# Subtracting a group mean, DMA-bound: adjacent groups loaded in 50688-byte pieces instead of one group at a time

## The chip, the cores and the metric

The kernel runs on one core of one Trainium2 chip. The metric is the device time of one execution in microseconds (us), as the median of several runs. Faster or slower needs 2%. The span of a profile is the profiled execution alone and lies 1.7 to 2.2 us under the device time of the same run in the cases quoted here.

## The reference

```python
x = randn(8, 4096, 2112)            # float32, 276.8 MB
x_r = x.reshape(8, 1024, 4, 2112)
pooled = x_r.mean(axis=2)           # mean of four adjacent rows
upsampled = repeat(pooled, 4, axis=1)
return x - upsampled
```

Every element is read once and written once, with about two additions an element in between.

## The kernel before

A group is four adjacent rows of 2112 floats, 33792 bytes. A tile holds one group in each of 128 partitions, 4.325 MB, and there are 64 tiles ("groups" from here on). Six slots of that size form a ring. SyncE issues the loads, ScalarE's queue issues the stores, VectorE computes. No tensor is multiplied.

```python
def reduce_tile(b, landed):
    rows = slots[b].rearrange("p (f d) -> p f d", f=STRIDE)
    s = s_ps if b % 2 else s_sb
    for f in range(1, STRIDE):                       # three additions, 128x2112
        first = rows[:, 0, :] if f == 1 else s[:]
        add = nc.vector.tensor_add(out=s[:], in0=first, in1=rows[:, f, :])
        # ... waits: the load for f == 1, the step before it otherwise
    sub = nc.vector.scalar_tensor_tensor(            # rows = rows - s / 4, 128x8448, in place
        out=rows, in0=s[:, None, :].to_broadcast([P, STRIDE, D]),
        scalar=-1.0 / STRIDE, in1=rows, op0=mult, op1=add)
    # ...

for k in range(n):                                   # n = 64
    b, lap = k % SLOTS, k // SLOTS                   # SLOTS = 6
    load = nc.sync.dma_start(out=slots[b][:], in_=xg[k * P:(k + 1) * P])
    if lap:
        load._wait_ge(store_sems[b], 16 * lap)       # the slot's last store has landed
    load.then_inc(load_sems[b], 16)
# ... VectorE: a loop over the slots ...
for k in range(n):
    b = k % SLOTS
    store = nc.scalar.dma_start(out=og[k * P:(k + 1) * P], in_=slots[b][:])
    store._wait_ge(done_sem, k + 1)
    store.then_inc(store_sems[b], 16)
```

Of the kernel before, what the change touches and what calls it, by code (L numbers as in the profile page):

```python
# [1 line left out]

# [4 lines left out]

STRIDE = 4
SLOTS = 6  # L10
PAD = 224


@with_exitstack
def kernel(
    ctx: ExitStack,
    tc: tile.TileContext,
    x: bass.AP,
    out: bass.AP,
):  # L20






    nc = tc.nc
    B, S, D = x.shape
    P = nc.NUM_PARTITIONS
    W = STRIDE * D  # L30
    G = (B * S) // STRIDE
    assert S % STRIDE == 0 and G % P == 0
    n = G // P

    xg = x.rearrange("b (g f) d -> (b g) (f d)", f=STRIDE)
    og = out.rearrange("b (g f) d -> (b g) (f d)", f=STRIDE)
    f32 = mybir.dt.float32

    pad_pool = ctx.enter_context(tc.tile_pool(name="pad", bufs=1))
    io_pool = ctx.enter_context(tc.tile_pool(name="io", bufs=1))  # L40
    sum_pool = ctx.enter_context(tc.tile_pool(name="sum", bufs=1))
    psum_pool = ctx.enter_context(
        tc.tile_pool(name="psum", bufs=1, space=bass.MemoryType.PSUM)
    )
    pad_pool.tile([P, PAD], f32, name="pad")
    slots = [io_pool.tile([P, W], f32, name=f"slot{b}") for b in range(SLOTS)]
    s_sb = sum_pool.tile([P, D], f32, name="s_sb")
    s_ps = psum_pool.tile([P, D], f32, name="s_ps")

    load_sems = [tc.alloc_semaphore(f"load{b}") for b in range(SLOTS)]  # L50
    store_sems = [tc.alloc_semaphore(f"store{b}") for b in range(SLOTS)]
    step_sem = tc.alloc_semaphore("step")
    done_sem = tc.alloc_semaphore("done")

    adds = STRIDE - 1

    def reduce_tile(b, landed):
        rows = slots[b].rearrange("p (f d) -> p f d", f=STRIDE)
        s = s_ps if b % 2 else s_sb
        done = b * adds  # L60
        for f in range(1, STRIDE):
            first = rows[:, 0, :] if f == 1 else s[:]
            add = nc.vector.tensor_add(out=s[:], in0=first, in1=rows[:, f, :])  # L63
            if f == 1:
                add._wait_ge(load_sems[b], landed)
            else:
                add._wait_ge(step_sem, done + f - 1)
            add.then_inc(step_sem)
        sub = nc.vector.scalar_tensor_tensor(  # L69
            out=rows,  # L70
            in0=s[:, None, :].to_broadcast([P, STRIDE, D]),
            scalar=-1.0 / STRIDE,
            in1=rows,
            op0=mybir.AluOpType.mult,
            op1=mybir.AluOpType.add,
        )
        sub._wait_ge(step_sem, done + adds)
        sub.then_inc(done_sem)

    assert SLOTS % 2 == 0  # L80
    laps, rest = divmod(n, SLOTS)
    with tc.tile_critical():  # L82
        for k in range(n):
            b, lap = k % SLOTS, k // SLOTS
            load = nc.sync.dma_start(out=slots[b][:], in_=xg[k * P:(k + 1) * P])
            if lap:
                load._wait_ge(store_sems[b], 16 * lap)
            load.then_inc(load_sems[b], 16)

        with nc.vector.Fori(0, laps) as lap:  # L90
            landed = nc.vector.to_reg(16 * lap + 16)
            for b in range(SLOTS):
                reduce_tile(b, landed)
            nc.vector.wait_ge(step_sem, SLOTS * adds).then_inc(step_sem, -SLOTS * adds)
        for b in range(rest):
            reduce_tile(b, 16 * (laps + 1))

        for k in range(n):
            b = k % SLOTS
            store = nc.scalar.dma_start(out=og[k * P:(k + 1) * P], in_=slots[b][:])  # L100
            store._wait_ge(done_sem, k + 1)
            store.then_inc(store_sems[b], 16)


    for k in range(n - SLOTS, n):
        total = nc.gpsimd.to_reg(16 * (k // SLOTS + 1))
        tc.keep_in_program_order(nc.gpsimd.wait_ge(store_sems[k % SLOTS], total))


# [1 line left out]
_INS = ['x']  # L111
_OUTS = [((8, 4096, 2112), 'float32')]


# [23 lines left out]
```

## Time and profile before

| | before |
|---|---|
| median time | 1284.73 us (5 runs, 1284.56 to 1285.19) |
| span of the profile | 1283.3 us |
| VectorE busy | 1026.5 us, 80% |
| bytes moved | 553.66 MB, mean 431 GB/s |
| a load lands after / a store lands after | 60.1 us / 43.5 us |

The page's groups of VectorE give the cost of its work (columns: line, engine, operation, operands, shapes, count, then total us, mean ns of one, and the idle time ahead of them with what ended it):

```profile
L69 DVE SCALAR_TENSOR_TENSOR slot<-s_sb,slot 128x8448 f32<-128x8448 f32 x32 | 286.7, 8958 | 1.1
...
L63 DVE TENSOR_TENSOR s_sb<-slot 128x2112 f32<-128x2112 f32 x32 | 75.5, 2358 | 123.7 <-DMA slot<-in_x_dram 123.7
```

One subtraction takes 8.96 us and one addition 2.36 us. Nearly all of VectorE's idle time stands ahead of the first addition of a group and is ended by a load. That is what a kernel looks like whose DMA sets the pace.

### The profile page before, as it was taken

Reading aid. Unit: us, or ns where it says so; the run is one execution under the profiler, and the core shown is the slowest. Engines: PE = TensorE matmul, PEld = TensorE weight load, DVE = VectorE, ACT = ScalarE, POOL = GpSimd, SP = SyncE. Lnnn points to the kernel's source line nnn. Section 1 sums busy time; section 2 is a strip of 40 time slices with the busy share of each in tenths; the row PEclk is TensorE's granted clock in tenths of the full one; section 3 lists DMA queues with packets and bytes.
Section 4 is the critical chain, followed back from the end, with each engine's and each line's share of the span. In section 5 each row is a group of like instructions: output and inputs, shape, how many; then the busy total and the mean of one; then the engine's idle time right before and its main releaser. Section 6 shows DMA issues by size and latency. Waiting matters only on the chain.

```text
span 1283.3 us, 483 instructions
## 1 busy us (share of the span) xinstructions
DVE 1026.5 (80%) x256; POOL 0.2 (0%) x4
## 2 busy tenths in 40 slices
DVE  5998788787887877878778787787877878878785
POOL 0000000000000000000000000000000000000000
DMA  9999999999999999999999999999999999999999
GB/s 404 420 436 429 434 437 434 427 437 436 427 436 437 434 427 437 436 427 436 437 433 428 437 436 426 437 437 433 428 437 434 428 437 437 432 429 437 434 427 404
DMA packets 18432, 553.66 MB, mean 431 GB/s; under 512 B 2048, under 2 KB 2048, under 8 KB 2048
## 3 DMA queue, kind: packets, MB, share of 16 engines
q1 hardware_dynamic: 9216, 276.83, 50.1%
q10 hardware_dynamic: 9216, 276.83, 50.0%
HBM read 276.82 MB, written 276.82 MB: 431 GB/s over the span
## 4 chain that ended last, share of the span: by engine, by line
DVE 73%; another core or an unknown queue 24%; DMA 1%; issue 1%; DVEq 0%; SPq 0%
DVE slot L69 38%; DVE s_ps L63 18%; DVE s_sb L63 18%; DMA slot<-in_x_dram 1%; DVEq L90 0%; SPq L133 0%; SPq L82 0%
## 5 line engine op out<-in xcount | busy, mean ns | idle before, releaser
L69 DVE SCALAR_TENSOR_TENSOR slot<-s_sb,slot 128x8448 f32<-128x8448 f32 x32 | 286.7, 8958 | 1.1
L69 DVE SCALAR_TENSOR_TENSOR slot<-s_ps,slot 128x8448 f32<-128x8448 f32 x32 | 286.6, 8957 | 1.1
L63 DVE TENSOR_TENSOR s_sb<-slot 128x2112 f32<-128x2112 f32 x32 | 75.5, 2358 | 123.7 <-DMA slot<-in_x_dram 123.7
L63 DVE TENSOR_TENSOR s_ps<-slot 128x2112 f32<-128x2112 f32 x32 | 75.7, 2367 | 112.1 <-DMA slot<-in_x_dram 112.1
L63 DVE TENSOR_TENSOR s_ps<-s_ps,slot 128x2112 f32<-128x2112 f32 x64 | 151.4, 2366 | 2.2
L63 DVE TENSOR_TENSOR s_sb<-s_sb,slot 128x2112 f32<-128x2112 f32 x64 | 150.9, 2358 | 2.2
L122 POOL MEMSET const-bfloat16-1.0<- 128x1 bf16 x1 | 0.1, 102 | 0.0
L122 POOL MEMSET const-uint8-127<- 128x1 uint8 x1 | 0.1, 102 | 0.0
L122 POOL MEMSET const-float32-0.0<- 128x1 f32 x1 | 0.1, 99 | 0.2 <-issue 0.2
L122 POOL MEMSET const-float32-1.0<- 128x1 f32 x1 | 0.1, 99 | 0.0
## 6 DMA issues: line engine op xcount, KB each, us to landing
slot<-in_x_dram SPq DMA_DIRECT2D x64, 4224.0 KB, 60.1
out_dram<-slot ACTq DMA_DIRECT2D x64, 4224.0 KB, 43.5
```

The lines of the kernel that those rows point to most:

```text
L63: add = nc.vector.tensor_add(out=s[:], in0=first, in1=rows[:, f, :])
L69: sub = nc.vector.scalar_tensor_tensor(out=rows, in0=s[:, None, :].to_broadcast([P, STRIDE, D]), scalar=-1.0 / STRIDE, in1=rows, op0=mybir ...
L122: nc = _bacc.Bacc("TRN2", target_bir_lowering=False, num_devices=1)
```

## The change

Intent: fewer and larger load transfers. The first 54 groups are taken as 18 blocks of three adjacent groups, so that a partition's data of a block is 12 contiguous rows, 101376 bytes. A block is loaded as two pieces of six rows (50688 bytes a partition), but stored a group at a time. A piece ends in the middle of the second group, so a load must wait for two groups' stores. The last ten groups go one at a time as before. The diff, cut to its core:

```diff
+BLOCK = 3
+BLOCKS = 18
-    slots = [io_pool.tile([P, W], f32, name=f"slot{b}") for b in range(SLOTS)]
+    ring = io_pool.tile([P, SLOTS * W], f32, name="ring")
 # ... the access patterns of a block: 12 rows a partition ...
+    def block(h, landed):
+        base = h * rows_all
+        s0, s1 = sums[h], sums[1 - h]
+        group(s0, base, (load_sems[h][0], landed)).then_inc(done_sem)
+        add(s1, ring_rows(base + 4, 1), ring_rows(base + 5, 1))
+        nc.vector.wait_ge(step_sem, steps.count)
+        add(s1, s1[:], ring_rows(base + 6, 1), (load_sems[h][1], landed))
+        add(s1, s1[:], ring_rows(base + 7, 1))
+        subtract(s1, base + 4, STRIDE).then_inc(done_sem)
+        group(s0, base + 8).then_inc(done_sem)
-        for k in range(n):
-            b, lap = k % SLOTS, k // SLOTS
-            load = nc.sync.dma_start(out=slots[b][:], in_=xg[k * P:(k + 1) * P])
-            if lap:
-                load._wait_ge(store_sems[b], 16 * lap)
-            load.then_inc(load_sems[b], 16)
+        for b in range(BLOCKS):
+            h, lap = b % 2, b // 2
+            for e in range(2):
+                q = h * BLOCK + 2 * e
+                if lap and e == 0:
+                    nc.sync.wait_ge(store_sems[q], 16 * lap)
+                load = nc.sync.dma_start(
+                    out=ring_rows(h * rows_all + e * piece, piece),
+                    in_=xb[b][:, e * piece * D:(e + 1) * piece * D],
+                )
+                if lap:
+                    load._wait_ge(store_sems[h * BLOCK + 1 + e], 16 * lap)
+                load.then_inc(load_sems[h][e], 16)
+        for k in range(singles):
+            # ... ten single groups, loaded as before ...
 # ... the stores: one a group, in both parts ...
```

More of the change, by code (lines that the diff above doesn't have):

```diff
@@ L32 @@
     assert S % STRIDE == 0 and G % P == 0
-    n = G // P
-    xg = x.rearrange("b (g f) d -> (b g) (f d)", f=STRIDE)
-    og = out.rearrange("b (g f) d -> (b g) (f d)", f=STRIDE)
     f32 = mybir.dt.float32
+    singles = G // P - BLOCK * BLOCKS
+    laps = BLOCKS // 2
+    assert BLOCKS % 2 == 0 and SLOTS == 2 * BLOCK and singles >= SLOTS
+    rows_all = BLOCK * STRIDE
+    piece = rows_all // 2
+    xr = x.rearrange("b s d -> (b s) d")
+    orow = out.rearrange("b s d -> (b s) d")
+    cut = BLOCKS * P * rows_all
+    xb = xr[0:cut].rearrange("(n p r) d -> n p (r d)", p=P, r=rows_all)
+    ob = orow[0:cut].rearrange("(n p r) d -> n p (r d)", p=P, r=rows_all)
+    xs = xr[cut:B * S].rearrange("(n p f) d -> n p (f d)", p=P, f=STRIDE)
+    os_ = orow[cut:B * S].rearrange("(n p f) d -> n p (f d)", p=P, f=STRIDE)
     pad_pool = ctx.enter_context(tc.tile_pool(name="pad", bufs=1))
@@ L45, with ring_rows, add, subtract @@
     pad_pool.tile([P, PAD], f32, name="pad")
-    slots = [io_pool.tile([P, W], f32, name=f"slot{b}") for b in range(SLOTS)]
+    ring = io_pool.tile([P, SLOTS * W], f32, name="ring")
     s_sb = sum_pool.tile([P, D], f32, name="s_sb")
     s_ps = psum_pool.tile([P, D], f32, name="s_ps")
-    load_sems = [tc.alloc_semaphore(f"load{b}") for b in range(SLOTS)]
-    store_sems = [tc.alloc_semaphore(f"store{b}") for b in range(SLOTS)]
+    sums = [s_sb, s_ps]
+    load_sems = [[tc.alloc_semaphore(f"load{h}{e}") for e in "eo"] for h in range(2)]
+    sload = [tc.alloc_semaphore(f"sload{q}") for q in range(SLOTS)]
+    store_sems = [tc.alloc_semaphore(f"store{q}") for q in range(SLOTS)]
     step_sem = tc.alloc_semaphore("step")
     done_sem = tc.alloc_semaphore("done")
-    adds = STRIDE - 1
-    def reduce_tile(b, landed):
-        rows = slots[b].rearrange("p (f d) -> p f d", f=STRIDE)
-        s = s_ps if b % 2 else s_sb
-        done = b * adds
-        for f in range(1, STRIDE):
-            first = rows[:, 0, :] if f == 1 else s[:]
-            add = nc.vector.tensor_add(out=s[:], in0=first, in1=rows[:, f, :])
-            if f == 1:
-                add._wait_ge(load_sems[b], landed)
-            else:
-                add._wait_ge(step_sem, done + f - 1)
-            add.then_inc(step_sem)
+    def ring_rows(first, count):
+        return ring[:, first * D:(first + count) * D]
+    class Steps:
+        count = 0
+    steps = Steps()
+    def add(s, a, b, wait=None):
+        ins = nc.vector.tensor_add(out=s[:], in0=a, in1=b)
+        if wait is not None:
+            ins._wait_ge(*wait)
+        else:
+            ins._wait_ge(step_sem, steps.count)
+        ins.then_inc(step_sem)
+        steps.count += 1
+    def subtract(s, first, count):
+        rows = ring_rows(first, count).rearrange("p (f d) -> p f d", f=count)
         sub = nc.vector.scalar_tensor_tensor(
             out=rows,
-            in0=s[:, None, :].to_broadcast([P, STRIDE, D]),
+            in0=s[:, None, :].to_broadcast([P, count, D]),
             scalar=-1.0 / STRIDE,
@@ L76, in reduce_tile @@
         )
-        sub._wait_ge(step_sem, done + adds)
-        sub.then_inc(done_sem)
-    assert SLOTS % 2 == 0
-    laps, rest = divmod(n, SLOTS)
-    with tc.tile_critical():
-        for k in range(n):
-            b, lap = k % SLOTS, k // SLOTS
-            load = nc.sync.dma_start(out=slots[b][:], in_=xg[k * P:(k + 1) * P])
-            if lap:
-                load._wait_ge(store_sems[b], 16 * lap)
-            load.then_inc(load_sems[b], 16)
+        sub._wait_ge(step_sem, steps.count)
@@ new lines, in subtract, with group @@
+        return sub
+    def group(s, first, wait=None):
+        add(s, ring_rows(first, 1), ring_rows(first + 1, 1), wait)
+        for f in range(2, STRIDE):
+            add(s, s[:], ring_rows(first + f, 1))
+        return subtract(s, first, STRIDE)
+    def block(h, landed):
[8 more added lines that the diff above has]
+        group(s0, base + 8).then_inc(done_sem)
@@ new lines @@
+    with tc.tile_critical():
+        for b in range(BLOCKS):
[12 more added lines that the diff above has]
+        for k in range(singles):
+            q, lap = k % SLOTS, k // SLOTS
+            load = nc.sync.dma_start(out=ring_rows(q * STRIDE, STRIDE), in_=xs[k])
+            load._wait_ge(store_sems[q], 16 * (laps + lap))
+            load.then_inc(sload[q], 16)
@@ L90 @@
         with nc.vector.Fori(0, laps) as lap:
             landed = nc.vector.to_reg(16 * lap + 16)
-            for b in range(SLOTS):
-                reduce_tile(b, landed)
-            nc.vector.wait_ge(step_sem, SLOTS * adds).then_inc(step_sem, -SLOTS * adds)
-        for b in range(rest):
-            reduce_tile(b, 16 * (laps + 1))
-        for k in range(n):
-            b = k % SLOTS
-            store = nc.scalar.dma_start(out=og[k * P:(k + 1) * P], in_=slots[b][:])
+            steps.count = 0
@@ new lines @@
+            for h in range(2):
+                block(h, landed)
+            nc.vector.wait_ge(step_sem, steps.count).then_inc(step_sem, -steps.count)
+        steps.count = 0
+        for k in range(singles):
+            q, lap = k % SLOTS, k // SLOTS
+            group(sums[k % 2], q * STRIDE, (sload[q], 16 * (lap + 1))).then_inc(done_sem)
+        for k in range(BLOCK * BLOCKS + singles):
+            q = k % SLOTS
+            b, g = divmod(k, BLOCK)
+            if b < BLOCKS:
+                rows = ob[b][:, g * W:(g + 1) * W]
+            else:
+                rows = os_[k - BLOCK * BLOCKS]
+            store = nc.scalar.dma_start(out=rows, in_=ring_rows(q * STRIDE, STRIDE))
@@ L101 @@
             store._wait_ge(done_sem, k + 1)
-            store.then_inc(store_sems[b], 16)
-    for k in range(n - SLOTS, n):
-        total = nc.gpsimd.to_reg(16 * (k // SLOTS + 1))
+            store.then_inc(store_sems[q], 16)
+    for k in range(singles - SLOTS, singles):
+        total = nc.gpsimd.to_reg(16 * (laps + k // SLOTS + 1))
         tc.keep_in_program_order(nc.gpsimd.wait_ge(store_sems[k % SLOTS], total))
```

## The prediction

> **What bounds the kernel now.** I read the page first: the busy share of each engine, then the DMA row of the 40 slices, then the queues.
>
> ```profile
> DVE 1026.5 (80%) x256; POOL 0.2 (0%) x4
> DMA  9999999999999999999999999999999999999999
> DMA packets 18432, 553.66 MB, mean 431 GB/s; under 512 B 2048, under 2 KB 2048, under 8 KB 2048
> q1 hardware_dynamic: 9216, 276.83, 50.1%
> q10 hardware_dynamic: 9216, 276.83, 50.0%
> ```
>
> VectorE, the only computing engine, has a fifth of the span free. The 16 DMA engines have nothing free: the load queue (q1) and the store queue (q10) hold 50.1% and 50.0% of their time. 276.83 MB must come in and 276.83 MB go out, whatever the order. So the first question is whether the DMA engines ever run below their rate. I asked for the busy time and GB/s of five stretches of the span (columns: stretch, its us, DVE busy, POOL busy, clock, DMA share, GB/s):
>
> ```profile
> 3.00:28.00 25.00, 14.57 (x4) 0.00 (x0) 1.00 1.00 433
> 28.00:36.00 8.00, 7.93 (x4) 0.00 (x0) 1.00 0.95 355
> 36.00:136.00 100.00, 90.77 (x23) 0.00 (x0) 1.00 1.01 435
> 136.00:1236.00 1100.00, 884.35 (x222) 0.00 (x0) 1.00 1.00 433
> 1236.00:1276.00 40.00, 28.84 (x7) 0.00 (x0) 1.00 1.00 433
> ```
>
> Loads alone (3 to 28 us) run at 433 GB/s, loads with stores (136 to 1236) at 433, and the last stretch, nearly all stores, at 433. The rate doesn't depend on which queue has work, only on some queue having it. The one weak stretch is 28 to 36 us, when the first store starts: 8 x (433-355)/433 = 1.4 us by this coarse count (a packet falls into one stretch or the next), about 1.0 us by the packet records. All bytes at 433 GB/s take 553.66/0.433 = 1279 us (1277 if the unrounded rate is 433.5). The span is 1283.3. So everything that is not bytes at full rate is worth 4 to 6 us, under 0.5%.
>
> The packet records show how two queues share an engine. In the steady part a packet is one partition's row of 33792 bytes and takes 1.251 us, with loads alone or mixed; each engine moves one at a time and strictly alternates load, store, load, store. So the share is per packet, not per byte.
>
> Last, the DMA issues and the waits of VectorE:
>
> ```profile
> slot<-in_x_dram SPq DMA_DIRECT2D x64, 4224.0 KB, 60.1
> out_dram<-slot ACTq DMA_DIRECT2D x64, 4224.0 KB, 43.5
> DVE s_sb L63 <- DMA slot<-in_x_dram: 123.7, 30, 13.3
> DVE s_ps L63 <- DMA slot<-in_x_dram: 112.1, 30, 3.8
> ```
>
> A load lands 60.1 us after issue and a store 43.5 us, while one group moves in and out in 2 x 4.325 MB / 0.433 = 20.0 us: three loads and two stores are always queued. VectorE takes 3 x 2.36 + 8.96 = 16.05 us a group, then waits 3.8 us for a load. 60.1 + 16.05 + 43.5 = 119.7 us is six periods of 20 us: all six slots are in use, and the DMA sets the period. The chain of waits (73% VectorE) misleads here: VectorE lies on it because each store follows a subtraction, but it has 3.8 us of slack a group.
>
> **What the Trainium skill says.** "DMA: Bandwidth & Descriptors", section "Bandwidth", gives a ceiling of 435.2 GB/s for the 16 engines; the trace sits at 433, 0.5% under it. Section "Queues, rings and completion order" of the same page says each engine takes turns between the queues that have work, at packet granularity; the trace agrees, 1.251 us turns of one row each. Section "Rules for kernel authors" asks for 128 partitions and at least 1 MiB a DMA; before already moves 4.3 MB, so there is little left to gain from size. Section "Latency and other measured facts" warns of HBM rows at large power-of-two pitches. The new pitch is 3 x 33792 = 101376 bytes, no power of two; no run yet shows whether it matters.
>
> **The change part by part.**
> 1. Instructions. VectorE keeps 192 additions and 64 subtractions of the same shapes, 64 x 16.05 = 1027 us, and the stores stay 64 of 33792 bytes a partition. Loads go from 64 to 36 + 10. The program order shows no other work.
> 2. Load packets. 18 blocks x 128 x 2 = 4608 rows of 50688 bytes replace 6912 of 33792: 2304 fewer, 144 an engine. The worth of one: a row repeats every 33792 x 16 / 433.5 GB/s = 1.247 us; at the skill's 435.2 it would be 1.242. So at most 0.005 us a row (an estimate from that ceiling), 144 x 0.005 = 0.7 us saved.
> 3. Start. The first load is 1.5 groups, so VectorE starts at about 18 us instead of 13.3 and the first store at 34 instead of 29.5. Four pieces (60 us of loading) are queued from the start, so the DMA stays busy: cost 0.
> 4. Steady part, worked by hand with 10 us for a group and 15 us for a piece alone. While both queues have work a load turn is 1.87 us and a store turn 1.25 us: the loads get 60%, a piece takes 25 us, and in those 25 us one group is stored. A piece needs two groups' stores done before it is issued (pieces share the middle group). From about 82 us a block goes: first piece beside one store, 25 us; second piece beside the next store, 25 us; then no slot is free and the third store runs alone, 10 us; then the next first piece. 25 + 25 + 10 = 60 us for three groups, exactly 3 x 20. VectorE needs 48.2 of these 60. In the hand schedule a block's stores are ready 16, 39 and 55 us after its first piece has landed, but their turns on the queue come 60 us or later after it, so the store queue never runs dry. The load queue does, once a block for some 10 us, and the stores fill it at 433 GB/s. Cost in bytes: 0.
> 5. End. Ten single groups run as before, at 50:50. More stores are queued behind the loads here (about five against three), so the last subtraction is hidden; before also has no hole there (433 GB/s to 1276 us). Gain: 0.
> 6. Restarts of the load queue. This is the only new thing. Before never lets a queue run empty, and the single time that a queue starts beside a busy one, at 28 to 36 us, each engine shows two load packets stretched from 1.25 to about 1.4 to 2.2 us, together about 1.0 us. After restarts the load queue once in each of 16 blocks. If every restart costs that, 16 x 1.0 = 16 us, fully on the path because the DMA is the bound. If that microsecond belongs to the very first store only, it is 0.
>
> Sum: 1284.7 - 0.7 + 0 = 1284 without a restart cost, 1284.7 - 0.7 + 16 = 1300 with it in full.
>
> **The rivals.** (a) Pure conservation of bytes: nothing moves, 1284 us. For it: the rate is 433 in every mix. (b) Restart cost: 1292 to 1300; if the second piece also comes too late and the queue empties twice a block, 16 + 16 = 32 us, 1316. The store beside a piece starts about 2 us before it (issue to first byte is 1.4 us in the trace), and so finishes before it and frees the next piece just in time; I hold twice a block unlikely. (c) Larger pieces starve VectorE, and VectorE then starves the stores: against it, 48.2 of 60 us busy, and a backlog of stores; each store is ready some 40 us before its turn, so VectorE would have to be that late. (d) Larger packets are faster than 0.005 us a row: the ceiling allows at most 0.5%, 1278 us. (e) The 101376-byte pitch slows HBM: the trace has nothing of it; I give it a few per cent.
>
> **Range and chances.** I give (a) a little more than half and (b) most of the rest, perhaps with a partial cost; between 1284 and 1300 I put 1288, with 1281.5 to 1303 for 8 in 10. Faster by 2% (under 1259 us) would need more than the ceiling: 0.5%. Slower by 2% (over 1310.4) needs the double restart or a pitch effect: 5.5%. Within 2%: 94%.
>
> **What would show it.** Right: VectorE still 1026 us busy; load rows of 50688 bytes at about 1.87 us; GB/s of 433 in nearly every slice, and over a block of 60 us; waits of VectorE on loads in two sizes a block, some 5 and 7 us by hand; the load queue empty once a block. Restart cost: short dips of GB/s every 60 us, with load rows above 1.9 us right after each gap. Wrong: DMA share below 9 in the steady part (a hole), a block period well over 61 us, or a store row longer than 1.25 us in the mix (the pitch).

## The result, and the profile after

| | before | after |
|---|---|---|
| median time | 1284.73 us | 1285.80 us (5 runs, 1285.16 to 1285.90) |
| span of the profile | 1283.3 us | 1283.6 us |
| VectorE busy | 1026.5 us | 1023.1 us |
| a store lands after | 43.5 us | 55.5 us |
| first data packet to last, packet records | 1280.1 us | 1280.2 us |

The ratio of after to before is 1.0006, 95% interval 0.9994 to 1.0018. A ratio here is the mean time of one kernel's fast runs over that of the other's fast runs of the same rounds, so it is not quite the ratio of the medians. One core can't show the difference between two dies, so a run counts as slow only if it is over 1.5% above the fastest of its kernel; nothing in the comparison of the two kernels rests on such runs.

The page of the changed kernel, its VectorE row, its GB/s in 40 slices, its packets and its two data queues:

```profile
DVE 1023.1 (80%) x256; POOL 0.2 (0%) x4
GB/s 404 413 441 435 426 433 438 430 442 428 440 424 444 434 423 434 440 429 431 437 432 443 421 435 437 431 432 436 433 440 430 440 428 428 434 436 434 430 434 394
DMA packets 15841, 553.66 MB, mean 431 GB/s; under 512 B 1760, under 2 KB 1760, under 8 KB 1760
q1 hardware_dynamic: 6624, 276.83, 50.0%
q10 hardware_dynamic: 9216, 276.83, 49.9%
```

The load queue q1 has 6624 packets in place of 9216 for the same megabytes, and yet the mean rate is again 431 GB/s. The two lowest slices, 404 and 394, are the first and the last: the transfers begin in the one and run out in the other, before and after alike. The stretches of the span, cut as for before (the start comes later, since the first piece is larger):

```profile
34.00:42.00 8.00, 7.86 (x4) 0.00 (x0) 1.00 0.99 372
136.00:1036.00 900.00, 719.26 (x180) 0.00 (x0) 1.00 1.00 433
1036.00:1236.00 200.00, 173.75 (x43) 0.00 (x0) 1.00 1.01 434
1236.00:1276.00 40.00, 16.05 (x4) 0.00 (x0) 1.00 1.00 433
```

The blocks (136 to 1036 us), the single groups and the end all run at 433 to 434 GB/s. The weak stretch at the first store is still there. One block in mid run, cut at its own phases by hand:

```profile
496.00:506.00 10.00, 7.56 (x3) 0.00 (x0) 1.00 1.00 433
506.00:531.00 25.00, 22.07 (x5) 0.00 (x0) 1.00 1.00 433
531.00:556.00 25.00, 18.32 (x5) 0.00 (x0) 1.00 1.00 433
556.00:566.00 10.00, 8.11 (x3) 0.00 (x0) 1.00 1.00 433
```

In the two 10 us stretches the packet records hold almost no load packet: the load queue is dry and stores move alone. In the two 25 us stretches loads and stores are mixed. The rate is 433 GB/s in all four. VectorE's timeline of the next block, only the rows at which it waits (start, us, engine, line, operation, and in brackets the idle time with what ended it):

```profile
532.98 2.37 DVE L74 TENSOR_TENSOR s_ps<-ring 128x2112 f32<-128x2112 f32 x1 [4.81 <-DMA ring<-in_x_dram]
...
557.83 4.75 DVE L74 TENSOR_TENSOR s_sb<-s_sb,ring 128x2112 f32<-128x2112 f32 x2 [6.42 <-DMA ring<-in_x_dram]
...
593.15 2.36 DVE L74 TENSOR_TENSOR s_sb<-ring 128x2112 f32<-128x2112 f32 x1 [5.51 <-DMA ring<-in_x_dram]
```

A block waits twice, 4.8 us for its first piece and 6.4 us for its second, and the next block begins 593.15 - 532.98 = 60.2 us later. The issues of the DMA with their median time to landing:

```profile
out_dram<-ring ACTq DMA_DIRECT2D x64, 4224.0 KB, 55.5
ring<-in_x_dram SPq DMA_DIRECT2D x36, 6336.0 KB, 33.3
```

Before, three loads and two stores were queued. After, little more than one load is queued (33.3 us from issue to landing, of which a piece's own moving takes 25), and the waiting has shifted to the store queue, 55.5 us. The data wait in the ring in either case; only the place has changed.

### The profile page after: what moved, and what is told of

Its sections match the earlier page's. It is cut to its first block, busy times and chain, and to the rows that moved or that the text cites. A ratio compares the mean times of both kernels' runs of the same rounds, so it can differ in the third digit from the quotient of the medians.

```text
span 1283.6 us, 495 instructions
## 1 busy us (share of the span) xinstructions
DVE 1023.1 (80%) x256; POOL 0.2 (0%) x4
## 3 DMA queue, kind: packets, MB, share of 16 engines
q1 hardware_dynamic: 6624, 276.83, 50.0%
q10 hardware_dynamic: 9216, 276.83, 49.9%
## 4 chain that ended last, share of the span: by engine, by line
another core or an unknown queue 80%; DVE 9%; DMA 7%; SPq 1%; issue 0%; DVEq 0%
DVE ring L84 5%; DMA out_dram<-ring 4%; DMA ring<-in_x_dram 4%; DVE s_ps L74 2%; DVE s_sb L74 2%; SPq L119 1%; SPq L128 0%; SPq L118 0%; DVEq L106 0%; SPq L182 0%; SPq L112 0%
## 5 line engine op out<-in xcount | busy, mean ns | idle before, releaser
L84 DVE SCALAR_TENSOR_TENSOR ring<-s_sb,ring 128x8448 f32<-128x8448 f32 x32 | 286.7, 8958 | 1.1
L84 DVE SCALAR_TENSOR_TENSOR ring<-s_ps,ring 128x8448 f32<-128x8448 f32 x32 | 286.6, 8957 | 1.1
L74 DVE TENSOR_TENSOR s_sb<-s_sb,ring 128x2112 f32<-128x2112 f32 x64 | 150.9, 2358 | 53.8 <-DMA ring<-in_x_dram 51.8
L74 DVE TENSOR_TENSOR s_ps<-s_ps,ring 128x2112 f32<-128x2112 f32 x64 | 151.4, 2366 | 52.8 <-DMA ring<-in_x_dram 50.8
L74 DVE TENSOR_TENSOR s_sb<-ring 128x2112 f32<-128x2112 f32 x32 | 75.3, 2352 | 69.9 <-DMA ring<-in_x_dram 69.9
L74 DVE TENSOR_TENSOR s_ps<-ring 128x2112 f32<-128x2112 f32 x32 | 75.6, 2362 | 51.5 <-DMA ring<-in_x_dram 51.5
## 6 DMA issues: line engine op xcount, KB each, us to landing
out_dram<-ring ACTq DMA_DIRECT2D x64, 4224.0 KB, 55.5
ring<-in_x_dram SPq DMA_DIRECT2D x36, 6336.0 KB, 33.3
```

Of the source, the lines that this page charges most:

```text
L74: ins = nc.vector.tensor_add(out=s[:], in0=a, in1=b)
L84: sub = nc.vector.scalar_tensor_tensor(out=rows, in0=s[:, None, :].to_broadcast([P, count, D]), scalar=-1.0 / STRIDE, in1=rows, op0=mybir. ...
```

## The experiments

All kernels below start from one of the two kernels with a single edit more that is common to all: the last wait of GpSimd is written on constants. Packet figures are from the packet records of the profiled run. "Stretched" is the time by which packets exceeded the normal duration of their size, summed and divided by 16 engines; "idle" is the time with fewer than 16 packets in flight, counted for each missing packet and also divided by 16. A gap of a queue is counted from the start of its last packet to the start of the next, so that one packet's own 1.25 or 1.87 us is in it. Both kernels have little of either in the whole run: before 1.6 us stretched and 1.2 us idle, after 1.9 and 1.5.

### The changed kernel again

```diff
-        total = nc.gpsimd.to_reg(16 * (laps + k // SLOTS + 1))
-        tc.keep_in_program_order(nc.gpsimd.wait_ge(store_sems[k % SLOTS], total))
+            nc.gpsimd.wait_ge(store_sems[k % SLOTS], 16 * (laps + k // SLOTS + 1))
```

> The changed kernel again; only the last wait of GpSimd is written on constants (the register form is not accepted by the safety check). Theory A (the time is the bytes at the rate of the DMA engines plus a fixed head and tail): 1284 to 1286.5 us, ratio to before 1.000 to 1.001. Rival B (the half microsecond to one microsecond by which the changed kernel was slower is real and steady): ratio 1.0005 to 1.0010 again, with a start and a tail that each lose 0.2 to 0.4 us more in the packet records. Load packets of 50688 bytes at 1.872 us, none stretched at the 31 restarts of the load queue.

Measured: 1285.43 us against 1284.81, ratio 1.0004 (0.9991 to 1.0017). The start lost 0.25 us idle and 0.76 us stretched, the end 0.60 us idle; before has 0.13, 0.60 and 0.57. The median is again above before, here by 0.6 us, but the interval holds 1. In all four comparisons of this schedule (the first, this one, and below 20 blocks and one more addition) it is 0.6 to 1.1 us above, and every interval holds 1: the sign is a hint and not a finding. The larger end (0.94 us idle in the first profile) did not come again. The restarts of the load queue again have no stretched packets to speak of. The control agrees with theory A, and leaves B open: the time is the bytes, and a difference of half a microsecond can't be told from none.

### Every row its own transfer

```diff
-            load = nc.sync.dma_start(out=slots[b][:], in_=xg[k * P:(k + 1) * P])
+            for f in range(STRIDE):
+                c = slice(f * D, (f + 1) * D)
+                load = nc.sync.dma_start(out=slots[b][:, c], in_=xg[k * P:(k + 1) * P, c])
 # ... the same for the stores; counts of 16 become 64
```

> Before, with every load and store cut in four transfers of one 8448-byte row a partition: 65536 packets in place of 16384, 3072 more an engine, the same bytes. Theory A with a fixed cost a packet: from the two sizes measured (1.251 us for 33792 bytes, 1.872 us for 50688) the fixed part is 3 x 1.251 - 2 x 1.872 = 0.009 us, so 3072 x 0.009 = 28 us more, 1312 us; with 0.005 us as predicted, 15 us more, 1300 us. Rival: no fixed cost a packet, 1285 us.

Measured: 1304.39 us, ratio 1.0151 (1.0136 to 1.0166). The page's packets and the mid run of this kernel:

```profile
DMA packets 73732, 553.71 MB, mean 425 GB/s; under 512 B 8192, under 2 KB 8192, under 8 KB 8192
...
136.00:1236.00 1100.00, 871.27 (x219) 0.00 (x0) 1.00 1.01 428
```

The loss is spread over the whole run (428 in place of 433 GB/s), with no hole. 1304.39 - 1284.81 = 19.6 us over 3072 more packets an engine is 0.0064 us a packet, between the two figures expected. It includes four times as many semaphore packets. It also includes about 3 us that lie at the start and the end: in the steady part alone (100 to 1230 us, 427.6 against 433.1 GB/s by the packet records) the loss comes to 16.4 us for all bytes, 0.0054 us a packet. So the prediction's saving of 144 packets an engine is worth 0.8 to 0.9 us.

### Stores as pieces too

```diff
+        for b in range(BLOCKS):
+            for e in range(2):
+                store = nc.scalar.dma_start(out=ob[b][:, e * piece * D:(e + 1) * piece * D],
+                                            in_=ring_rows(h * rows_all + e * piece, piece))
+                store._wait_ge(done_sem, b * BLOCK + 2 + e)
 # ... and a load waits for the one store of its piece
```

> The changed kernel with its 18 blocks also stored as two 50688-byte pieces, so each load waits for one store. Theory A: 2304 fewer store packets, 144 an engine, at 0.005 to 0.009 us: 0.7 to 1.3 us less than the changed kernel, 1284 to 1285 us, no hole in the DMA row. Rival C (a store of a piece must wait for two groups, and the coarser stores starve the DMA): GB/s below 425 in slices of the steady part, 1300 us or more.

Measured: 1290.89 us median of six runs, but they are 1286.40, 1286.57, 1287.68, 1294.10, 1300.20 and 1302.35; ratio 1.0072 (1.0035 to 1.0109). The profiled run is one of the quick ones, 1286.57 us: 434 GB/s from 136 to 1036 us, no hole there, and 2.3 us idle at 1270 to 1273 us, where the last store waits for the last subtraction, which ends at 1272.1 us. Neither expectation came out. The saving did not show, and the profile can't say what the runs near 1300 us did. That stays open. It also shows that one program can vary by over 1% from run to run, which bears on the single runs below.

### One load at a time

```diff
+            if k:
+                nc.sync.wait_ge(load_sems[(k - 1) % SLOTS], 16 * ((k - 1) // SLOTS + 1))
             load = nc.sync.dma_start(out=slots[b][:], in_=xg[k * P:(k + 1) * P])
```

> Before, with each load issued only when the load ahead of it has landed, so the load queue runs empty 63 times while stores go on. Theory A (a queue may run empty as long as the other has work): 1285 to 1295 us, the upper end if both queues are sometimes empty at once. Rival D (each restart of a queue costs the engines about 1 us, as at the first store): 63 us more, about 1348 us, with stretched load packets after each gap.

Measured: 1354.55 us (1349.15 to 1362.98), ratio 1.0528 (1.0502 to 1.0554); the profile is of the slowest of the four runs, 1362.98. My theory missed, and the number is the rival's. The issues in the page show what I had overlooked:

```profile
slot<-in_x_dram SPq DMA_DIRECT2D x64, 4224.0 KB, 20.3
out_dram<-slot ACTq DMA_DIRECT2D x64, 4224.0 KB, 19.4
```

Not only the load queue but the store queue too is down to one transfer (19.4 us to landing against 43.5), so that both run dry again and again. The profiled run's 77.6 us between first and last packet beyond before split into 49.7 us stretched (51.3 - 1.6) and 27.6 us idle (28.8 - 1.2, of which 10.9 lie at the end, where nothing hides the last subtraction and store). The largest clusters of stretched packets, 1.2 to 1.35 us an engine each, lie some 4 us after a store has started, where the next load joins it; others are smaller; in the changed kernel 16 long restarts have next to none. So a restart can cost what rival D said, but does not always.

### The store queue drained three times

```diff
+            if k in (16, 32, 48):
+                nc.scalar.wait_ge(store_sems[(k - 1) % SLOTS], 16 * ((k - 1) // SLOTS + 1))
             store = nc.scalar.dma_start(out=og[k * P:(k + 1) * P], in_=slots[b][:])
```

> Before, with stores 16, 32 and 48 held until the store ahead of each has landed: the store queue runs empty three times in mid run while loads go on. Rival D for the store queue (a start of the store queue beside running loads costs about 1 us whenever it happens): at each of the three, load packets stretched beyond 1.3 us, in sum about 1 us an engine. Theory E (the microsecond at the first store belongs to the first use only): no stretched packets at the three, and time within 0.3% of before.

Measured: 1290.57 us in its one run, whose state is unknown, beside 1284.75; 0.45%, more than the 0.3% allowed. The three restarts of the store queue, after 5.6, 6.8 and 6.7 us without a store packet, show no stretched packet at the restart itself. But after the third, from 1016 to 1225 us, single packets, nearly all of them loads, are stretched here and there, 3.0 us in sum, and the end has 1.9 us idle. So rival D falls for these three, and theory E does not explain the rest.

### A small load and a small store ahead of the first big one

```diff
+        first = nc.scalar.dma_start(out=pad[:], in_=xg[0:P, 0:PAD])       # after group 0 has landed
+        second = nc.scalar.dma_start(out=og[0:P, 0:PAD], in_=pad[:])      # after group 1 has landed
         for k in range(n):
             store = nc.scalar.dma_start(out=og[k * P:(k + 1) * P], in_=slots[b][:])
```

> Before, with two small transfers on the store queue ahead of the first big store: a load of 224 columns into the unused pad when the first group has landed (about 13 us), then a store of it, which the first group's store overwrites later, when the second group has landed (about 23 us). Theory E: the stretched load packets move to the first use of the queue at about 13 us (if any first use counts) or to the small store at about 23 us (if the first write counts), and the first big store has none. Rival D: stretched packets again at the first big store, about 1 us an engine, because the queue is empty again by then.

Measured: stretched load packets at the first big store as ever, 0.74 us an engine, and none above 0.1 us at the two small transfers. Theory E, first use of the queue or first write, falls. The time was a surprise, 1320.38 us in its one run, whose state is unknown. Its GB/s row:

```profile
GB/s 400 427 428 439 424 424 425 427 420 428 432 424 424 422 423 425 423 424 427 421 423 423 424 425 417 424 417 422 420 419 422 417 423 420 416 425 420 424 427 295
```

From about 100 us to the end the rate is some 423 in place of 433 GB/s, with all engines busy; packets are stretched all along, 23.9 us for loads and 2.3 for stores, and at the end the 16 engines finish 14 us apart (1303.3 to 1317.0 us; before, 0.8 us). Whether the two short transfers caused that is not shown: it is a single run, and the kernel with stores as pieces varied by 16 us with no change at all.

### More blocks, fewer single groups

```diff
-BLOCKS = 18
+BLOCKS = 20
 # ... and the assertion that there are at least six single groups goes
```

> The changed kernel with 20 blocks and 4 single groups at the end in place of 18 and 10. Theory A: the last stores are queued behind each other either way, so 1284 to 1286.5 us and 433 GB/s until the last slice. Rival F (the ten single groups are needed for the end: with blocks nearer to the end the last subtractions are laid bare): 5 to 20 us more and a dip in the last two slices.

Measured: 1285.43 us against 1284.75, ratio 1.0006 (0.9989 to 1.0023). With four single groups the end is as full as with ten, so rival F falls: the number of single groups doesn't matter here. The load queue now restarts 18 times after a long gap, and the packets stretched after the start come to next to nothing.

### Four slots

```diff
-SLOTS = 6
+SLOTS = 4
```

> Before with four slots in place of six. Theory A: four slots allow 4 x 20 = 80 us from the issue of a load to the landing of its store; a group needs at least 20 us for each transfer at half the rate, 16 us of VectorE and some 4 us of issue and landing, about 60 us: 1284 to 1287 us. Rival C (buffers in flight are what keeps the rate): slower by over 2%, 1310 us or more, with slices below 425 GB/s.

Measured: 1289.73 us, ratio 1.0036 (1.0019 to 1.0052). The steady part is 433 GB/s as expected; then comes the end:

```profile
136.00:1236.00 1100.00, 883.05 (x221) 0.00 (x0) 1.00 1.00 433
1236.00:1280.00 44.00, 32.09 (x8) 0.00 (x0) 1.00 0.91 394
```

About 3.7 us are idle after 1270 us because fewer stores are queued to cover the last subtraction, and 1.3 us more are stretched. Four slots carry the rate, but not the end. The theory held for the steady part, and its number missed by 3 us because I had not counted the end.

### VectorE made slower

```diff
         add(s, ring_rows(first, 1), ring_rows(first + 1, 1), wait)
+        for _ in range(1):        # 2 in the second kernel
+            add(s, ring_rows(first, 1), ring_rows(first + 1, 1))
 # ... the same for a block's second group, and in the kernel before
```

> The changed kernel with the first addition of each group done twice (same result): VectorE 64 x 2.36 = 151 us busier, 18.4 us a group, 55.3 us of the 60 us a block. Theory A: 1285 to 1287 us, the waits for loads shrink instead. Rival G (VectorE and its waits lie on the path, as the chain of waits of before has it): up to 151 us more, 1436 us.

> The changed kernel with the first addition of each group done three times: 20.8 us of VectorE a group, above the 20.0 us of the DMA. Theory A: VectorE becomes the bound, 18 + 64 x 20.8 + 11 = 1360 us, DMA share below 9.5 tenths. Rival: unchanged at 1286 us if VectorE had more slack than the 20 us period says.

> Before with the first addition of each group done twice: 18.4 us of VectorE a group against 20.0 us of DMA. Theory A: 1284 to 1287 us. Rival G: up to 151 us more, 1436 us.

Measured: the changed kernel with one more addition 1285.61 us, ratio 1.0003 (0.9987 to 1.0020); with two 1369.03 us, ratio 1.0654 (1.0633 to 1.0676), 9 us above the 1360 expected; the kernel before with one more 1290.30 us median of 1285.03, 1287.09, 1293.51 and 1294.88, ratio 1.0048 (1.0011 to 1.0085), 3 us above what was expected. The changed kernel with one and then with two more additions, busy time of VectorE:

```profile
DVE 1173.5 (91%) x320; POOL 0.2 (0%) x4
```

```profile
DVE 1323.4 (97%) x384; POOL 0.2 (0%) x4
```

150 us more VectorE work cost nothing in the changed kernel. The next 150 us took VectorE's need per group to 20.8 us, above the DMA's 20.0, and it became the bound: 1323.4 us of work, 18.8 us until the first load has landed, and the rest for the last store and the gaps between instructions. Rival G, VectorE on the path, falls. The kernel before is less steady under the same load, in its four runs; its store queue holds less (46.2 us to landing, against 53.1). That this is the reason is not shown, since the profile is of a quick run, 1287.09 us.

### The block schedule with smaller load packets

```diff
-                load = nc.sync.dma_start(
-                    out=ring_rows(h * rows_all + e * piece, piece), ...)
+                cuts = (0, 4, 6) if e == 0 else (6, 8, 12)
+                for c0, c1 in zip(cuts, cuts[1:]):
+                    load = nc.sync.dma_start(
+                        out=ring_rows(h * rows_all + c0, c1 - c0),
+                        in_=xb[b][:, c0 * D:c1 * D])
 # ... the wait only on the first of the two; counts of 16 become 32
```

> The changed kernel with each load piece cut in two transfers, of 4 and 2 rows of 8448 bytes (33792 and 16896 bytes a partition), issued together under the same wait: the load queue runs dry and restarts once a block as in the changed kernel, with several stores queued, but with packets no larger than in the kernel before. Theory H (a restart is free when the other queue has several transfers waiting; the size of the packet has no part in it): no stretched packets at the restarts; 36 x 128 / 16 = 288 more packets an engine at the 0.0064 us that the run with 8448-byte rows gives (19.6 us for 3072) is 1.8 us more than the changed kernel, 1286 to 1289 us. Rival J (it is the large packet that keeps the restart free, since loads of 33792 bytes that joined running stores were stretched in the kernel with one load at a time): about 1 us for each of 16 restarts, 1300 us or more, stretched packets after each gap of the load queue.

Measured: 1326.44 us (1325.92 to 1332.88), ratio 1.0322 (1.0305 to 1.0340); the profile is of the slowest of the five runs, 1332.88. Both theories missed: H in its time, J in its cause. The issues, and the stretches at 433 GB/s in the changed kernel:

```profile
out_dram<-ring ACTq DMA_DIRECT2D x64, 4224.0 KB, 25.3
ring<-in_x_dram SPq DMA_DIRECT2D x46, 4224.0 KB, 47.5
ring<-in_x_dram SPq DMA_DIRECT2D x36, 2112.0 KB, 50.3
```

```profile
136.00:1036.00 900.00, 690.64 (x174) 0.00 (x0) 1.00 0.99 422
1036.00:1236.00 200.00, 166.79 (x42) 0.00 (x0) 1.00 1.00 424
1236.00:1316.00 80.00, 61.98 (x16) 0.00 (x0) 1.00 0.87 376
```

The waiting has gone from the store queue (55.5 us to 25.3) to the load queue (33.3 to about 50). A load packet is now 33792 or 16896 bytes, 25344 on average, and against a store packet of 33792 the loads get 25344 / (25344 + 33792) = 43% of the bytes while both queues have work, where the changed kernel's 50688 gave them 60%. Counted in the packet records wherever both queues move (100 to 1030 us), it is 44% here and 63% in the changed kernel. Worked by hand from these shares, a piece takes 15 / 0.43 = 35 us beside stores in place of 25, during which two groups are stored and not one. The backlog of stores is used up and VectorE gets its data late and in bursts. The records agree: store packets are absent for over 3 us 15 times (up to 17.8 us), in the changed kernel 5 times (up to 3.9 us). The 47.4 us from first to last packet beyond the changed kernel split into 29.1 us more idle (30.6 - 1.5), 16.6 us more stretched (18.5 - 1.9) and 288 x 0.0064 = 1.8 us for the packets, 47.5 in sum. Of the idle time, 19 us lie in the last 40 us of the run. One engine is 8.7 us behind the other 15 there (it ends at 1329.5 us, they by 1320.9), and before that those 15 idle for some 9 us while VectorE subtracts the last group, with no store left to move meanwhile. In how far the other four runs had such an end is not recorded. The edit also doubles the number of load transfers, so that the size of the packet as the cause of the lost backlog is the reading that fits, by the arithmetic of the shares, and not one that a second edit has isolated. Rival J's bound of 1300 us or more is met, but the load queue had only 7 gaps over 3 us, the longest 3.7 us, so that 16 restarts of it can't be the cause.

## Why the prediction was right or wrong

The time, 1285.8 us, lies in the range, 2.2 us under the 1288 predicted, and "within 2%" was right.

**What bounds the kernel** held: bytes at 433 GB/s before and after, and VectorE could be given 150 us more work for nothing.

**Instructions (step 1)** held: VectorE 1023.1 us busy, stores unchanged.

**Load packets (step 2).** Rows of 50688 bytes took 1.872 us, as expected (1.87). The saving of 0.7 us was about right in size (0.8 to 0.9 us by the run with small rows), but it does not show in the time. Between first and last packet the two kernels differ by 0.1 us, and the records say where the saving went: the start lost 0.2 us more stretched (1.80 against 1.59) and 0.2 more idle (0.30 against 0.13), the end 0.4 us more because the engines finish less together (0.94 against 0.57), and some 0.1 us of late stretched packets. These are single profiles, so it is an account of two runs, not a law; in the control's profile the end lost no more than before's. Why the medians differ by 1.1 us, while the spans of the profiled runs differ by 0.3, is within the interval and not settled.

**Start (step 3).** First load at 18.8 us (predicted 18), first store at 35.0 (34).

**Steady part (step 4).** The hand schedule was right nearly to the microsecond: 60.2 us a block against 60, phases of 25, 25 and 10 us, waits of 4.8 and 6.4 us against "some 5 and 7", 433 GB/s in each phase. It rests on loads getting 60% of the bytes by packet size, and the experiment that changed only the transfers and their size lost the schedule.

**End (step 5).** It held: stores move alone for the last 47 us against 30 before, and the number of single groups plays no part.

**Restarts of the load queue (step 6).** Here the prediction chose between 0 and 16 us and put the point 4 us above the lower sum. The load queue did run dry just 16 times, for 9.5 to 13.8 us from packet start to packet start (7.7 to 11.9 us with no load packet at all). After the start all stretched packets together come to 0.1 us, so the term measured 0. The reason offered for that branch, "belongs to the very first store only", is half right: a small store ahead did not take the microsecond away from the first big store, and three later drains of the store queue had none at the restart. But the one-load kernel shows about 50 us of stretched packets, so "a restart is free" is not a rule either. What decides it is not settled. What is shown is that it was free in the 16 long restarts of the changed kernel, where stores were queued behind one another.

**The rivals.** (a) is what happened. (c), a starved VectorE, did not happen here, but the kernel with cut pieces shows that the block schedule could have tipped into it. The margin I gave (some 40 us of stores queued) fits the 55.5 us from a store's issue to its landing, but I had not said how much it depends on the packet sizes. (b) came in neither form. One reading behind it was wrong: the 1.4 us from issue to first byte is not in the trace of before, which has 1.0 us for the first load (0.95 to 1.96 us) and 4.1 us for the first store (29.50 to 33.59). In the changed kernel it was 3.6 us for a load at the block shown (504.2 to 507.8). That did no harm: the second piece of this block was issued at 523.5 us, 8 us before the first had moved its last packet, so the queue did not empty twice a block. (d) and (e) did not show: the rate is 433 GB/s again, and a stored row takes 1.251 us as before.

No version beat the kernel before. The 20-block kernel has the shortest stretch from first to last packet, 1279.3 us against 1280.1, and a median of 1285.43 us that is not faster.

## What to carry to other kernels

When 16 DMA engines are busy from start to end at one rate whatever the mix, larger transfers have only the cost of the packets saved to give: here at most 0.0064 us each, under a microsecond in 1285. Before re-cutting transfers, work out by hand which queue gets what share of the bytes. Here two busy queues shared them about as their packet sizes did (63% for loads of 50688 bytes beside stores of 33792, 44% for smaller ones), and the schedule that lived on a backlog (stores that cover a dry load queue) was lost in the one run that changed the ratio. When checking, look at the time to landing of each queue as well as at the GB/s, since it shows where the slack sits.

## What the Trainium skill lacked or had wrong

- "DMA: Bandwidth & Descriptors", section "Queues, rings and completion order", has the turns at packet granularity, which the traces bear out (in the steady part before, load and store packets alternate on each engine, one every 1.247 us), but not the consequence for two queues with packets of unequal size: packets of 50688 against 33792 bytes left a block at 60.2 us, and load packets of 33792 and 16896 bytes in the same schedule took the store queue from 55.5 to 25.3 us and the time to 1326 us.
- The same page, section "Where 436 GB/s comes from", says that for HBM to SBUF transfers "the HBM side (~358) binds". On the one core running here loads and stores moved 433 GB/s. Taken alone the sentence misleads for a single core; the same page's measured 425 GB/s for 16 MB, which it marks as a single-core number, fits.
- No page tells what makes packets take longer than others of their size: they were stretched by 26 us in sum (423 GB/s) in the one run with two small transfers at the start, by 51 us with one load at a time, and next to none at 16 restarts of the load queue in the changed kernel. The runs here don't settle the cause.
